# Eight single orders in a hand-scheduled transformer block: query copies, first scores, last probabilities, first casts of up and down, sums near the end

## The chip, the cores and the metric

The kernel is one program on one core of a Trainium2 chip. The time is that of a whole execution on the device, in microseconds (us); of several executions the median is taken. The engines are TensorE (PE, matrix products into PSUM banks), VectorE (DVE), ScalarE (ACT), GpSimd (POOL) and SyncE (SP, which issues most of the DMA transfers). Each runs its own list of instructions in order and waits on semaphores for the others.

## The reference

One layer of a diffusion backbone over 512 latent tokens of width 2048, with 256 context tokens, all in float32:

```python
h = modulate(rms_norm(x), sh_a, sc_a)                    # the context likewise
q_a, kv_a, k_rope, gate_b, gate_c, hc = split(h @ w_in)
q = rope(rms_norm(q_a) @ w_q_b)                          # 8 heads of 128 + 64
k, v = rms_norm(kv_a) @ w_kv_b                           # latent and context tokens
att = softmax(q @ k.T * scale) @ v                       # 512 rows against 512 + 256 keys
conv = gate_b * dwconv3(gate_c * hc)
x = x + gt_a * (group_rms_norm(concat(att, conv)) @ w_out)
h = modulate(rms_norm(x), sh_f, sc_f)
a, g = split(dwconv3(h @ w_up))                          # 2 x 5504 columns
x = x + gt_f * ((a * silu(g)) @ w_down)
return rms_norm(x, g_final)
```

## The kernel before

**Numbers.** PE takes float32 in a rounded form (fp32r). So each factor is split into a high and a low part, and a product is three matmuls: high by high, high by low, low by high (`mm3`, L202 to L204; `mm2`, L210 to L212, takes two factors that lie side by side). Such a split (`split`, `split4`, `hilo`) is a cast of ACT, named with an h at its end (`wk0h`, `dw00h`), and a subtraction of DVE, named with an l (`wk0l`, `dw00l`), which needs the cast. A matmul of L202 waits for the cast, that of L204 (low weights) or L203 (low data) for the subtraction. The casts' buffers rotate: a new one waits until PE has read an old one.

**Stages**, one after the other: the input projection (0 to 384 us of the trace), the attention (384 to 612), the output projection (612 to 790), the first product of the MLP, "up" (790 to 1647), and the second, "down" (1647 to the end). Up and down are done with seven products of blocks instead of eight, so sums of weight blocks are made first (DVE, and DMAs of POOL that add to what lies there).

**Order.** Each engine's order is set when the program is built: a scheduler places the instructions by its own costs, in the order in which the code was written where nothing else speaks. `tc.issue_after(i)` asks, without a wait at run time, that what is written under it comes later than `i` on the engine of `i`. `keep` holds written order, and the list `behind` puts the first matmul of the next `mm3` after a given one. `bg`, `drain` and `pump` run side work piece by piece.

**PSUM in the attention.** `sml` gives one of four single banks, `big` one of two pairs of banks. Scores of one step (one head, 128 rows) fill a pair (`scores`, L1012 to L1025: five matmuls of 512 columns over the latent keys and five of 256 over the context keys). `softmax` takes the minimum on DVE (`mn`, L1035) and the exponential on ACT (`p`, L1038), which frees the pair. `transposes` (L1043) turns the probabilities with PE in two halves (`t`, L1053; three 128-column matmuls each), and splits them into `pth` (ACT, L1056) and `ptl` (DVE, L1057). `attend` multiplies these by the values (`po`). `s02` is the score tile of head 0, step 2; `pth` and `ptl` carry no step in the profile. `rms` (L359) normalizes the context's keys: sums of squares over partitions by two one-column matmuls from `kct` (L343), a square root, a reciprocal, a spread by transposes (L324) and a copy `kcr` (L356), in one pair of banks from `big`.

**Side work there.** `q_nope`, `q_rope`, `k_nope`, `values` prepare the next pair of heads; `xq` (L934) is the copy of the queries that are rotated (`qr`, L409), `wk` and `wv` the split weights of keys and values. `late_both` (L1127) does dot products of the modulation on DVE (L281). `gb` are spreads of the convolution's norms, merged by DVE (`acc`, L404). After the loop, `out_row` (L1202) splits the first mixed rows (`mx`) and starts the output projection (`of`).

**First rows of up.** `first_weights` (`ufw0` to `ufw5`) and `hf_tile` (L1257 on) make the factors of the first products `uf`. `hf_early` (L1278) makes those of the first half of the tokens for the rows 0 to 2 as side work of the last output column `ol`. A second norm (`rms_steps` over `fq`) runs beside them.

**First weights of down.** `finish` (L1543) does the last two products `q4` and `q3` of a column group of up. After the last group (42) down begins: it splits `dw00` and multiplies it with `yl0`, read back by SP (`y_load`) in a high and a low part, into the banks `d00` to `d07`.

**Last groups of down.** `weights_of` (L1646) loads four blocks of a group and adds them (`v23s`, L1660; a POOL DMA, L1661, adds a fourth block). `d_p2` (L1718) ends with two sums, `a11` and `a12` (L1722, L1723), from which the weights of the product `p6` are cast; `d_q4` and `d_q3` are the last products of the group before, `ended` its end. Groups are numbered 0 to 23: `v21q4` are weights of group 21, `v23s` a sum of group 23.

## Time and profile before

| what | value |
|---|---|
| time, median of 3 runs | 2112.55 us (2111.74 to 2114.03) |
| the profiled execution's own time | 2109.51 us |
| its span, first to last instruction | 2107.7 us |
| granted TensorE clock, mean | 0.998 |
| PE busy | 2080.4 us (99%) |
| DVE busy | 1792.8 us (85%) |
| ACT busy | 1100.6 us (52%) |
| POOL busy | 126.8 us (6%) |
| DVE busy from 384 to 612 us | 178.21 of 228 us |

A row of the timeline gives the start, the duration, the engine, the line, the operation, what it writes and reads and, in brackets, how long the engine was idle before it and who ended that. Names stand without buffer numbers there: `s` is any score tile, `hf` any split row. Rows merged into one say how many (x2). A matmul's duration holds a pipeline of which the next one overlaps a part, so the spacing of two starts tells more than the duration: 512 columns start 0.23 us apart, 256 columns 0.12 us. The list of waits sums idle time by the pair of instructions, that which waited and that which ended it.

### The profile page before, as it was taken

The numbers are of one execution on the slowest core, as the hardware profiler recorded it, in microseconds if no ns is written. First come the engines' busy times: TensorE is split into PE (matmuls) and PEld (weight loads), VectorE is DVE, ScalarE is ACT, GpSimd is POOL, SyncE is SP. The second block draws the span as 40 slices with busy tenths as digits, with TensorE's granted clock in tenths as the row PEclk, the third lists the DMA queues.
The fourth block names the chain that finished last, engine by engine and source line by source line (L and its number), as shares of the span: only waits on it lengthen the run. The fifth ranks groups of instructions, "written<-read, shape, count | busy, mean of one in ns | idle before, by whom it ended". The sixth has DMA issues, their size and how long they took to land.

```text
span 2107.7 us, 35339 instructions
## 1 busy us (share of the span) xinstructions
PE 2080.4 (99%) x13304; PEld 1875.2 (89%) x13304; DVE 1792.8 (85%) x2911; ACT 1100.6 (52%) x1815; POOL 126.8 (6%) x161
## 2 busy tenths in 40 slices
PE   8999999999999999999999999999999999999997
PEld 6787888888888889999999999999999889999997
DVE  7888987788777879898999899999999659888887
ACT  6675454655552237555555555555555333333445
POOL 0000000000000000110000000000000000000000
PEclk9999999999999999999999999999999999999999
DMA  9899997445538966677888878888888989878684
GB/s 336 295 342 323 326 331 256 138 144 194 195 140 326 346 222 181 168 217 207 243 227 229 243 221 236 244 226 229 241 227 232 362 302 315 251 231 240 202 247 135
DMA packets 166606, 514.78 MB, mean 244 GB/s; under 512 B 18722, under 2 KB 23074, under 8 KB 157346
## 3 DMA queue, kind: packets, MB, share of 16 engines
q1 hardware_dynamic: 127744, 407.90, 56.4%
q0 software_dynamic: 19312, 70.40, 15.7%
q10 hardware_dynamic: 19378, 34.23, 4.3%
q8 instruction: 104, 1.70, 0.3%
q14 instruction: 68, 0.55, 0.1%
HBM read 465.26 MB, written 46.14 MB: 243 GB/s over the span
## 4 chain that ended last, share of the span: by engine, by line
PE 87%; DVE 5%; DMA 4%; issue 2%; ACT 2%; POOL 0%; DVEq 0%; POOLq 0%; ACTq 0%; SPq 0%
PE pp L202 3%; PE pp L204 3%; PE pp L203 3%; DMA rw<-in_w_in 2%; PE o L202 1%; PE o L204 1%; PE o L203 1%; PE d L202 1%; PE d L203 1%; PE d L204 1%; PE uf L202 1%; PE uf L203 1%; PE uf L204 1%; PE of L202 1%; PE of L204 1%
## 5 line engine op out<-in xcount | busy, mean ns | idle before, releaser
L1460 POOL DMA_DIRECT2D u_s<-in_w_up x80 | 68.4, 855 | 680.5 <-DMA u_s<-in_w_up 405.2
L285 DVE SCALAR_TENSOR_TENSOR ada<-ada,sv 128x2048 f32<-128x2048 f32 x33 | 75.4, 2285 | 7.0 <-DMA ada<-in_w_ada 6.7
L671 DVE SCALAR_TENSOR_TENSOR ada<-ada,svc 128x1024 f32<-128x1024 f32 x64 | 77.1, 1217 | 2.8 <-DMA ada<-in_w_ada 2.8
L181 ACT CAST w_0h<-rw 128x512 fp32r<-128x512 f32 x50 | 30.7, 620 | 69.5 <-PE pp L203 33.5
L1581 DVE TENSOR_TENSOR u<-u,u_s 128x1024 f32<-128x1024 f32 x40 | 48.7, 1218 | 3.5 <-DMA u_s<-in_w_up 3.4
L256 DVE SCALAR_TENSOR_TENSOR ada<-ada,sv 128x1024 f32<-128x1024 f32 x40 | 48.3, 1217 | 3.2 <-DMA ada<-in_w_ada 3.2
L1582 DVE TENSOR_TENSOR u<-u,u 128x1024 f32<-128x1024 f32 x40 | 48.6, 1215 | 0.0
L182 DVE TENSOR_TENSOR w_0l<-rw,w_0h 128x512 fp32r<-128x512 f32 x50 | 34.0, 685 | 8.5 <-ACT w_0h L181 7.7
L1380 DVE TENSOR_TENSOR tp<-a,tp 128x256 fp32r<-128x256 f32 x90 | 37.4, 416 | 2.8 <-ACT tp L1379 2.8
L1035 DVE TENSOR_REDUCE mn<-s 128x1 f32<-128x768 f32 x32 | 30.5, 952 | 10.9 <-PE s L1024 10.9
L1379 ACT CAST tp<-a 128x256 fp32r<-128x256 f32 x90 | 35.7, 403 | 6.3 <-DMA yl6h<-y_d 3.7
L1085 POOL TENSOR_TENSOR gr<-gr,half 128x8 f32<-128x8 f32 x4 | 10.3, 2580 | 474.9 <-DVE gr L1084 427.8
L281 DVE SCALAR_TENSOR_TENSOR ra<-ra,sv 128x1024 f32<-128x1024 f32 x32 | 38.0, 1216 | 0.0
L1056 ACT CAST pth<-t 128x384 fp32r<-128x384 f32 x64 | 28.6, 485 | 16.8 <-PE t L1053 16.6
L1343 ACT ACTIVATE g<-g 128x512 f32<-128x512 f32 x43 | 27.3, 634 | 17.8 <-DVE g L1337 17.5
L1057 DVE TENSOR_TENSOR ptl<-t,pth 128x384 fp32r<-128x384 f32 x64 | 33.1, 547 | 3.3 <-ACT pth L1056 3.3
L1335 ACT ACTIVATE g<-cg,sm 128x512 f32<-128x512 f32 x40 | 32.6, 815 | 0.0
L1335 ACT ACTIVATE a<-ca,sm 128x512 f32<-128x512 f32 x40 | 32.1, 802 | 0.0
L683 ACT COPY acc<-pp 128x512 f32<-128x512 f32 x49 | 28.3, 580 | 5.3 <-PE pp L204 5.3
L1038 ACT ACTIVATE p<-s,mn 128x768 f32<-128x768 f32 x32 | 29.3, 915 | 3.2 <-DVE mn L1035 3.2
L1336 DVE SCALAR_TENSOR_TENSOR g<-cg,sm,g 128x511 f32<-128x511 f32 x40 | 29.8, 745 | 0.0
L1336 DVE SCALAR_TENSOR_TENSOR a<-ca,sm,a 128x511 f32<-128x511 f32 x40 | 29.8, 744 | 0.0
(10502 smaller groups left out, 8997.6 us busy)
## 6 DMA issues: line engine op xcount, KB each, us to landing
ada<-in_w_ada SPq DMA_DIRECT2D x128, 512.0 KB, 6.1
u<-in_w_up SPq DMA_DIRECT2D x120, 512.0 KB, 9.1
w<-t_d SPq DMA_DIRECT2D x161, 256.0 KB, 5.4
u_s<-in_w_up SPq DMA_DIRECT2D x80, 512.0 KB, 3.9
u_s<-in_w_up POOLq DMA_DIRECT2D x80, 512.0 KB, 9.8
ada<-in_w_ada SPq DMA_DIRECT2D x33, 1024.0 KB, 6.3
t_d<-tp ACTq DMA_DIRECT2D x126, 256.0 KB, 6.0
v<-in_w_dnw SPq DMA_DIRECT2D x72, 384.0 KB, 5.6
```

The lines of the kernel that those rows point to most:

```text
L202: PE.matmul(ps, w[0], x[0], start=first, stop=False, skip_group_check=on_top)
L203: PE.matmul(ps, w[0], x[1], start=False, stop=False, skip_group_check=on_top)
L204: PE.matmul(ps, w[1], x[0], start=False, stop=last, skip_group_check=on_top)
L256: ins = V.scalar_tensor_tensor(out=r, in0=r, scalar=1.0, in1=vec[:, i * 1024:(i + 1) * 1024], op0=ALU.mult, op1=ALU.mult, accum_out=col[:, ...
L281: keep(V.scalar_tensor_tensor(out=halves[i], in0=halves[i], scalar=1.0, in1=svs[i], op0=ALU.mult, op1=ALU.mult, accum_out=lc[:, t % 4:t % ...
L285: keep(V.scalar_tensor_tensor(out=r, in0=r, scalar=1.0, in1=sv, op0=ALU.mult, op1=ALU.mult, accum_out=mod[:, t:t + 1]))
L671: keep(V.scalar_tensor_tensor(out=raw[q], in0=raw[q], scalar=1.0, in1=svc[:, q * 1024:(q + 1) * 1024], op0=ALU.mult, op1=ALU.mult, accum_o ...
L1335: A.activation(u, src, AF.Identity, bias=s("fb", m), scale=s("fw", 86 + m))
L1336: V.scalar_tensor_tensor(out=u[:, 1:], in0=src[:, :T - 1], scalar=s("fw", m), in1=u[:, 1:], op0=ALU.mult, op1=ALU.add)
L1460: G_.dma_start(r[-1], src[more], accum_op=ALU.add)
L1581: V.tensor_tensor(out=a11, in0=a11, in1=s1, op=ALU.add)
L1582: V.tensor_tensor(out=a12, in0=a12, in1=a11, op=ALU.add)
```

## The change

No arithmetic is changed. Eight places get another order:

1. First scores, (a): the context keys' norm takes a single bank (`one=width < T`) instead of a pair. (b): `late_both` is written after the first softmax. (c): the next head pair's first product `q_nope(1, 0)` is put behind the last matmul of the second score tile.
2. Copies of rotated queries: `drain()` is put behind the first copy `xq0`, and in later pairs the splits of `wk` and `wv` behind the copy before them.
3. A side piece of the step n = 31 is put behind the last `ptl`.
4. Last probabilities: the first four `out_row` are put behind the last `pth` and `ptl`.
5. First casts of up: row 2 (`hf_tile(2, H0)`) leaves the side work and goes behind the first two splits of weights.
6. First cast of down: the split `dw00` is made inside the last `finish`, between its product `q4` and the activation that follows.
7. Sums near the end: for group 23, the sum `v23s` and its DMAs are written after `d_q4` of group 21,
8. and the two sums of group 22 as well as the end of a group before (`ended`) after that.

```diff
@@ -357,7 +357,7 @@
         yield pb[:, :width]
 
     def rms(sqs, n, width, dst):
-        for _ in rms_steps(sqs, n, 0, width, dst):
+        for _ in rms_steps(sqs, n, 0, width, dst, one=width < T):
             pass
 
     def hilo(src, n, nm, width=512):
@@ -931,13 +931,13 @@
                 Q[2 * pr + i] = hilo(ps, T, f"q{pr}{i}")
                 return
             xq = t2([P, T], F32, f"xq{pr}")
-            A.copy(out=xq, in_=ps)
+            xq_copied[:] = [A.copy(out=xq, in_=ps).ins]
             if pr:
                 q_rope(pr, xq)
             else:
                 q_rope_0.append(xq)
 
-        q_rope_0 = []
+        q_rope_0, xq_copied = [], []
 
         def q_rope(pr, xq):
             rope(xq, sml(f"qr{pr}"), f"qr{pr}")
@@ -952,8 +952,9 @@
         def k_nope(pr, i):
             if i == 0:
                 raw = wkv["kv"]
-                wkv["k"] = split(raw, 0, 512, f"wk{pr}")
-                wkv["v"] = split(raw, 512, 512, f"wv{pr}")
+                with tc.issue_after(xq_copied[0]) if pr else ExitStack():
+                    wkv["k"] = split(raw, 0, 512, f"wk{pr}")
+                    wkv["v"] = split(raw, 512, 512, f"wv{pr}")
             w = wkv["k"]
             psl = sml(f"pkl{pr}{i}")
             for k in range(2):
@@ -1009,6 +1010,8 @@
             return [(q_nope, pr, 0), (q_nope, pr, 2), (k_nope, pr, 0), (q_nope, pr, 1), (k_nope, pr, 1),
                     (values, pr, 0), (values, pr, 1), (values, pr, 2)]
 
+        scored = []
+
         def scores(st):
             hd, tt = st
             kl, kcx = K[hd]
@@ -1021,7 +1024,7 @@
                 PE.matmul(d, qh[:, tsl], klo, start=False, stop=False)
                 PE.matmul(d, ql[:, tsl], kh, start=False, stop=False)
                 PE.matmul(d, QR[hd][:, tsl], rh_, start=False, stop=False)
-                PE.matmul(d, QR[hd][:, tsl], rl_, start=False, stop=True)
+                scored[:] = [PE.matmul(d, QR[hd][:, tsl], rl_, start=False, stop=True).ins]
             return ss
 
         den, oo, PT = {}, {}, {}
@@ -1038,7 +1041,7 @@
             A.activation(pt, ss[:, :768], AF.Exp, bias=mn, scale=-1.0, accum_out=den[hd // 2][:, i:i + 1])
             return pt
 
-        ptl_last = []
+        pth_last, ptl_last = [], []
 
         def transposes(st, pt):
             hd, tt = st
@@ -1053,7 +1056,7 @@
                     PE.transpose(tr[:, kb * P:(kb + 1) * P], pt[:, (3 * u + kb) * P:(3 * u + kb + 1) * P], ident)
                 trv = tr[:, :384].rearrange("p (k t) -> p k t", k=3)
                 hi = pth[:, 3 * u:3 * u + 3, bs]
-                A.copy(out=hi, in_=trv)
+                pth_last[:] = [A.copy(out=hi, in_=trv).ins]
                 ptl_last[:] = [V.tensor_tensor(out=ptl[:, 3 * u:3 * u + 3, bs], in0=trv, in1=hi.bitcast(F32), op=ALU.subtract).ins]
 
         def attend(hd, half):
@@ -1107,7 +1110,8 @@
             q_nope(0, i)
         q_rope(0, q_rope_0[0])
         bg.extend(ctx_prep(g) for g in range(CTX_EARLY, 8))
-        drain()
+        with tc.issue_after(xq_copied[0]):
+            drain()
         bg.extend(post)
         for i in range(3):
             ctx_tile(i)
@@ -1124,11 +1128,12 @@
         late_load(ada_raw)
         for f, i in ((k_ctx, 0), (k_ctx, 1), (values, 2)):
             f(0, i)
-        late_both(ada_raw)
         out_raw = {}
         steps = [(hd, tt) for hd in range(NH) for tt in range(4)]
         ss = [scores(steps[0]), scores(steps[1])]
         pt = softmax(steps[0], ss[0])
+        late_both(ada_raw)
+        behind.append(scored[0])
         q_nope(1, 0)
         fetch(1, 1)
         for g in late_bg[:4]:
@@ -1150,7 +1155,8 @@
                 merge(n // 8 - 1)
             late_dot(1)
             if n > 24 and n % 2:
-                deque(late_bg[4 + (n - 25) // 2], 0)
+                with tc.issue_after(ptl_last[0]) if n == 31 else ExitStack():
+                    deque(late_bg[4 + (n - 25) // 2], 0)
 
             at = n % 8
             if at == 0 and n and n < 24:
@@ -1206,7 +1212,8 @@
         for k in range(OUT_EARLY):
             if k % 2 == 0:
                 w = row_weights(w_out_first, k, "of", raw=out_raw[k])
-            out_row(k, w)
+            with tc.issue_after(pth_last[0]), tc.issue_after(ptl_last[0]):
+                out_row(k, w)
         merge(3)
         drain()
 
@@ -1276,7 +1283,7 @@
         hf_last[:] = hf_last[1], ins.ins
 
     def hf_early():
-        for j in range(3):
+        for j in range(2):
             hf_tile(j, HS[0])
             yield
 
@@ -1475,6 +1482,8 @@
         residual(NK - 1, ps, HS[1])
     one_bank[0] = in_turn([6])
     bg.append(rms_steps(fsq, D, T // 2, T // 2, rl, wait=(1, 1), one=True, pin=True))
+    with tc.issue_after(first_two[0]), tc.issue_after(first_two[1]):
+        hf_tile(2, H0)
     held += [first_weights(k, k > 2) for k in range(2, EARLY)]
     with tc.issue_after(first_two[0]), tc.issue_after(first_two[1]):
         for k in range(3, EARLY):
@@ -1540,9 +1549,10 @@
         A.copy(out=r, in_=ps[:, :256])
         return r
 
-    def finish(st):
+    def finish(st, between=lambda: None):
         f, a22, s4, u2, u3, pa, pc, cg, ca = st
         product(pa, a22, "4", f"u{f}q4", False)
+        between()
         A.activation(ca[:, H0], pa[:, :256], AF.Identity, scale=-1.0)
         beside(ca[:, H0], pa, True)
         product(pc, s4, "22", f"u{f}q3", False)
@@ -1595,7 +1605,12 @@
         if first_acts:
             acts(*first_acts.pop(0))
         pend = f, a22, a12, u2, u3, pa, pc, cg, ca
-    finish(pend)
+    dw = {}
+
+    def down_first():
+        dw[0, 0] = split4(fetched.popleft(), 1024, "dw00")
+
+    finish(pend, down_first)
 
 
     phc.close()
@@ -1643,7 +1658,7 @@
     class Step:
         pass
 
-    def weights_of(st):
+    def weights_of(st, whole=True):
 
         z = Step()
         z.st, z.win, z.m = st, window(st), 2 * (st % 8)
@@ -1657,9 +1672,15 @@
         SP.dma_start(z.a11, src[0])
         SP.dma_start(z.s1, src[2])
         SP.dma_start(z.a12, src[1])
-        V.tensor_tensor(out=z.s3, in0=z.a11, in1=z.s1, op=ALU.add)
-        G_.dma_start(z.s1, src[3], accum_op=ALU.add)
-        SP.dma_start(z.a22, src[3])
+
+        def rest():
+            V.tensor_tensor(out=z.s3, in0=z.a11, in1=z.s1, op=ALU.add)
+            G_.dma_start(z.s1, src[3], accum_op=ALU.add)
+            SP.dma_start(z.a22, src[3])
+
+        z.rest = rest
+        if whole:
+            rest()
         return z
 
     y_load(0)
@@ -1671,7 +1692,7 @@
             plain_fetch()
             if h == 0 and k + 2 < STD:
                 y_load(k + 2)
-            w = split4(fetched.popleft(), 1024, f"dw{h}{k}")
+            w = dw.pop((h, k), None) or split4(fetched.popleft(), 1024, f"dw{h}{k}")
             for i in range(8):
                 mm3(ps[i], part(w, i), y[k], k == 0, k == STD - 1)
             pump(1)
@@ -1715,9 +1736,13 @@
         seven(z, z.pa, z.a11, "11", "p1", True)
         into(z, 0, H0, z.pa)
 
-    def d_p2(z):
+    def d_p2(z, sums=True):
         seven(z, z.pb, z.a12, "21", "p2", True)
         into(z, 0, H0, z.pb)
+        if sums:
+            d_sums(z)
+
+    def d_sums(z):
         with tc.issue_after(last_lo[0]):
             V.tensor_tensor(out=z.a11, in0=z.a11, in1=z.s1, op=ALU.add)
         V.tensor_tensor(out=z.a12, in0=z.a12, in1=z.a11, op=ALU.add)
@@ -1819,18 +1844,23 @@
                 win_load(*first.pop(0)) if first else None
         if prev is not None:
             d_q3(prev)
-            ended(prev)
+            if st < STEPS - 3:
+                ended(prev)
             if prev.st in (STEPS - 6, STEPS - 5):
                 j = 2 * (prev.st - STEPS + 6)
                 with tc.issue_after(last_hi[0]):
                     scaled[0][j] = scale_out(j, 0, True)
         d_p7(z)
-        prev = z
-
-    za, zb = nxt, weights_of(STEPS - 1)
+        before, prev = prev, z
+
+    za, zb = nxt, weights_of(STEPS - 1, False)
     d_p1(za)
-    d_p2(za)
+    d_p2(za, False)
     d_q4(prev)
+    with tc.issue_after(last_lo[0]):
+        zb.rest()
+        ended(before)
+    d_sums(za)
     d_p1(zb)
     d_p2(zb)
     d_p6(za)
```

What the scheduler makes of it is read from the lists of instructions. First PE, where the first scores are prepared: `pkl` are keys of a head, `pv` values, `rs<-io,kct` the sums of squares of the context's norm, `s` score tiles. Before:

```order
L995 MATMUL pv_3991<-wv0h,kl0h 128x256
L996 MATMUL pv_3991<-wv0l,kl0h 128x256
L343 MATMUL rs<-io,kct 128x1 x2
L997 MATMUL pv_3991<-wv0h,kl0l 128x256
L995 MATMUL pv_3991<-wv0h,kl1h 128x256
L996 MATMUL pv_3991<-wv0l,kl1h 128x256
L997 MATMUL pv_3991<-wv0h,kl1l 128x256
L1020 MATMUL s_4059<-kl00h,q00h 128x512
```

And now, at the place of the same two matmuls:

```order
L203 MATMUL pkl_3934<-kl1l,wk0h 128x512
L204 MATMUL pkl_3934<-kl1h,wk0l 128x512
L343 MATMUL rs<-io,kct 128x1 x2
L202 MATMUL pkl_3955<-kl0h,wk0h 128x512
L203 MATMUL pkl_3955<-kl0l,wk0h 128x512
L204 MATMUL pkl_3955<-kl0h,wk0l 128x512
L202 MATMUL pkl_3955<-kl1h,wk0h 128x512
```

The two matmuls stood shortly before the first scores; now they stand 26 rows further up, behind the six matmuls of the first key tile.

Then PE a little later, at the end of the fourth score tile: `s_4182` is `s03`, `t_4170` and `t_4176` are the transposed probabilities of step 1 (those of step 0, `t_4139` and `t_4145`, stood ahead of `s03` before), `pq` is a product of side work, `s_4246` is `s10`. Before:

```order
L1022 MATMUL s_4182<-kcx_4023,q00l 128x256
L1023 MATMUL s_4182<-krc,qro0h 128x256
L1024 MATMUL s_4182<-krc,qro0h 128x256
L1053 MATMUL t_4170<-io,p_4135 128x128 x3
L1053 MATMUL t_4176<-io,p_4135 128x128 x3
L202 MATMUL pq_4197<-qa0h,wq12h 128x512
L203 MATMUL pq_4197<-qa0l,wq12h 128x512
```

And now:

```order
L1026 MATMUL s_4182<-krc,qro0h 128x256
L1027 MATMUL s_4182<-krc,qro0h 128x256
L1056 MATMUL t_4139<-io,p_4078 128x128 x3
L1056 MATMUL t_4145<-io,p_4078 128x128 x3
L1056 MATMUL t_4170<-io,p_4135 128x128 x3
L1056 MATMUL t_4176<-io,p_4135 128x128 x3
L1023 MATMUL s_4246<-kl01h,q01h 128x512
```

Both steps' transposes now follow `s03` directly, and `s10` follows them without the 12 matmuls of `pq` between. On ACT the exponential `p02`, which frees the pair of banks for `s10`, stands behind the two casts `pth` of step 0 in both lists.

Last DVE, near the end: `c11` is a running sum of the result, `v2211` and `v2212` the sums `a11` and `a12` of group 22, `ssq` sums of squares for the last norm. Before:

```order
L1722 TENSOR_TENSOR v2211_22124<-v2211_22124,v22s1_22125 128x768
L384 TENSOR_TENSOR ssq_17429<-ssq_17429,eq80_22290 128x512
L1660 TENSOR_TENSOR v23s3_22324<-v2311_22321,v23s1_22322 128x768
L1708 SCALAR_TENSOR_TENSOR c11_18119<-v21a_22135,gn_95,c11_18119 128x256
L1723 TENSOR_TENSOR v2212_22126<-v2212_22126,v2211_22124 128x768
L1329 TENSOR_TENSOR v21q4l_22384<-v2122_21928,v21q4h_22383 128x768
```

And now:

```order
L1729 SCALAR_TENSOR_TENSOR c11_18119<-v21a_22135,gn_95,c11_18119 128x256
L1336 TENSOR_TENSOR v21q4l_22373<-v2122_21928,v21q4h_22372 128x768
L1677 TENSOR_TENSOR v23s3_22318<-v2311_22315,v23s1_22316 128x768
L384 TENSOR_TENSOR ssq_17433<-ssq_17433,eq80_22400 128x512
L1747 TENSOR_TENSOR v2211_22124<-v2211_22124,v22s1_22125 128x768
```

The subtraction `v21q4l` moved ahead of `v23s3` and of both sums of group 22. `v23p1l`, `v23p2l`, `v2311` and `v22p6l`, which come later, keep their order among themselves, but two of the moved operations (a `ssq` and `v2212`) now stand between `v23p1l` and `v23p2l`.

## Prediction

> **What bounds the kernel now.** I read the page's head first, then the clock, then the list of waits of PE, and then the timeline at each place where the change touches a wait.
>
> ```profile
> PE 2080.4 (99%) x13304; PEld 1875.2 (89%) x13304; DVE 1792.8 (85%) x2911; ACT 1100.6 (52%) x1815; POOL 126.8 (6%) x161
> core 0: 2107.7 us, clock 0.998
> ```
>
> PE is busy for all but 27.3 us of the span, and the clock is whole. The change removes no matmul, so it can only win where PE stands still, and it loses where it makes PE stand still. Only the waits that PE itself shows count; an order that is better for DVE or ACT and ends no wait of PE is worth nothing. Four of those that the eight edits may touch are these (us in total, times, longest):
>
> ```profile
> PE qr L409 <- ACT xq L934: 1.7, 2, 1.0
> PE v21a L204 <- DVE v21q4l L1329: 0.9, 1, 0.9
> PE s L1020 <- ACT p L1038: 0.7, 2, 0.5
> PE uf L202 <- ACT ufw0h L1328: 0.7, 1, 0.7
> ```
>
> Three more, of 0.46, 1.09 and 1.02 us, stand in rows below. Together that is 6.6 us, 0.31% of the time. A measurement of this kernel can tell about 0.2% (4.2 us) from no change. So even a full success is only just visible, and each place must be asked what is late next.
>
> A wait also costs a restart: below, the first matmul after one starts 0.34 us before its follower, where two such matmuls without a wait are 0.23 apart. I add 0.11 us to each wait that goes or comes. [...]
>
> **First scores.**
>
> ```profile
> 416.83 0.39 PE L202 MATMUL pkl<-kl0h,wk0h 128*128 128x512 f32 x1
> 417.06 0.40 PE L203 MATMUL pkl<-kl0l,wk0h 128*128 128x512 f32 x1
> 419.05 0.43 DVE L384 TENSOR_TENSOR kct<-kct,kc 128x256 f32<-128x256 f32 x1 [0.47 <-ACT kc L383]
> 424.90 0.50 PE L1020 MATMUL s<-kl00h,q00h 128*128 128x512 f32 x1 [0.46 <-ACT kcr L356]
> 425.24 0.40 PE L1021 MATMUL s<-kl00l,q00h 128*128 128x512 f32 x1
> ```
>
> Two waits go: the pair of banks no longer waits for the norm's copy `kcr` (0.46), and `s02` now follows `pq10` and three spreads, so that `p00` is done in time (0.5, the longer of the two waits for `p` in the list). With two restarts that is -1.2 us.
>
> Two come. The norm's two matmuls now follow the six of the first key tile: PE is there at 416.83 + 6 x 0.233 = 418.23, but `kct` ends at 419.05 + 0.43 = 419.48, on lists of ACT and DVE that are the same up to there. That is 1.25 + 0.11 = +1.36 us.
>
> The second is `s10`. Its pair of banks is freed by `p02`, which stands on ACT behind both casts `pth` of step 0:
>
> ```profile
> 437.83 0.86 ACT L1056 CAST pth<-t 128x384 fp32r<-128x384 f32 x2 [0.66 <-PE t L1053]
> 439.55 0.90 ACT L1038 ACTIVATE p<-s,mn 128x768 f32<-128x768 f32 x1 [0.86 <-DVE mn L1035]
> 440.35 0.19 ACT L1038 ACTIVATION_READ_ACCUMULATOR p<-s,mn 128x1 f32 x1
> 439.72 0.82 PE L1053 MATMUL t<-io,p 128*128 128x128 f32 x6
> ```
>
> From the start of the transposes, the first of them needs about 0.35 us, the casts 0.86, `p` and its reading 0.99: 2.2 us. PE has 12 transposes until `s10`, at 0.109 each (my spacing from the row of six: 0.82 less the last one's own 0.27, by 5) 1.3 us. The wait is 0.9 + 0.11 = +1.0 us. Before, `pq12` (12 matmuls of 512 columns, 2.8 us) covered it. The place as a whole: +1.36 + 1.0 - 1.2 = +1.2 us; from -1.2 (neither wait comes) to +1.6.
>
> **Copies of rotated queries.** There are two waits, of 1.0 and 0.7 us. The first, `xq0`, is to be met by putting `drain()` behind the copy; but the lists of ACT and of PE around it are the same row by row, so I give it nothing. For the second:
>
> ```profile
> 493.42 0.62 ACT L181 CAST wk2h<-rk 128x512 fp32r<-128x512 f32 x1 [1.93 <-DMA rk<-in_w_kv]
> 494.47 0.58 ACT L934 COPY xq<-pq 128x512 f32<-128x512 f32 x1
> 495.10 0.70 PE L409 MATMUL qr<-xq,kc 128*128 128x512 f32 x1 [0.70 <-ACT xq L934]
> ```
>
> ACT idled 1.93 us for the DMA with the copy queued behind. Now the copy comes first, in that idle time, and `wk2h` still starts when its data is there. -0.8 us, from -0.8 to -0.6.
>
> **Last probabilities.**
>
> ```profile
> 604.17 0.62 ACT L366 CAST mx0h<-acc 128x512 fp32r<-128x512 f32 x1
> 604.68 0.86 ACT L1056 CAST pth<-t 128x384 fp32r<-128x384 f32 x2
> 606.09 1.02 DVE L1057 TENSOR_TENSOR ptl<-t,pth 128x384 fp32r<-128x384 f32 x2
> 606.69 0.39 PE L203 MATMUL po<-ptl,v30h 128*128 128x256 f32 x1 [1.09 <-DVE ptl L1057]
> ```
>
> On ACT the casts `pth` now stand ahead of `mx0h`, on DVE `ptl` ahead of `acc` and `mx0l`. The first cast ends at 604.17 + 0.48 = 604.65 and the first `ptl`, 0.55 long with its handover, at 605.2: L203 starts at 605.25 instead of 606.69, -1.44 us. What is pushed back, `mx0h` to 605.6 and `mx0l` to 606.9, is needed by `of` at about 608.2. -1.45 us, from -1.6 to -0.9. The order given to the piece at n = 31 hides in DVE's idle time: 0.
>
> **First casts of up.**
>
> ```profile
> 791.21 0.83 ACT L1328 CAST ufw0h<-ufr 128x768 fp32r<-128x768 f32 x1
> 791.46 0.48 DVE L1287 SCALAR_TENSOR_TENSOR x<-ol,mod,x 128x256 f32<-128x256 f32 x1 [0.89 <-PE ol L204]
> 798.79 0.40 ACT L1248 CAST hf<-x 128x256 fp32r<-128x256 f32 x1
> 799.25 0.74 PE L202 MATMUL uf<-hf,ufw_0h 128*128 128x256 f32 x4
> ```
>
> With row 2 gone from ahead of it, `ufw0h` is done 1.4 us earlier and the wait of 0.7 goes. But in the rows before, PE reaches row 3 (`hf`, L1248) at 799.25, just after its cast ends at 799.19: the next limit is already there. Row 2's work now stands on ACT and DVE between 793.6 and 796.8. ACT's chain starts, as before, from the last column of `ol` at 791.46, and adding up its casts in the new order puts the end of row 3's cast at 799.2 again. DVE, which had made row 2's parts in idle time, is 0.3 us later there, while the two transposes of the second norm now fall into PE's wait (0.2 us). So what PE wins at 791 it waits for in front of row 3: 0 us, from -0.8 to +0.4.
>
> **First cast of down.**
>
> ```profile
> 1643.91 1.05 ACT L1328 CAST u42q3h<-u 128x1024 fp32r<-128x1024 f32 x1 [0.38 <-PE u42c L211]
> 1646.76 1.05 ACT L1328 CAST dw00h<-d 128x1024 fp32r<-128x1024 f32 x1 [1.79 <-PE u42a L203]
> 1647.86 0.50 PE L202 MATMUL d<-yl0h,dw00h 128*128 128x512 f32 x1 [1.02 <-ACT dw00h L1328]
> 1641.26 0.38 SPq L1641 DMA_DIRECT2D yl0h<-y_d  x1
> yl0l<-y_d SPq DMA_DIRECT2D x1, 256.0 KB, 5.7
> ```
>
> The two casts change places, and so buffers: `dw00h` comes at 1643.91, `u42q3h` at 1646.76, still 6 us ahead of its product. PE could go on 1.02 + 0.11 earlier, at 1646.73; `yl0h`, if it takes as long as `yl0l`, the load behind it, lands at 1641.26 + 5.7 = 1646.96. So -0.9 us. On SP, a load for group 0 now stands ahead of the loads of `yl5` and waits for the subtraction `dw05l`:
>
> ```profile
> 1671.40 1.22 DVE L1329 TENSOR_TENSOR dw05l<-d,dw05h 128x1024 fp32r<-128x1024 f32 x1 [1.16 <-ACT dw05h L1328]
> yl5h<-y_d SPq DMA_DIRECT2D x1, 256.0 KB, 6.4
> 1681.55 0.63 PE L202 MATMUL d<-yl5h,dw05h 128*128 128x512 f32 x2
> ```
>
> That ends 0.9 us earlier, at 1671.7; three loads later, at an estimated 0.5 us each, `yl5h` is issued at 1673.2 and lands at 1679.6, 1.0 us before its use, which is also 0.9 earlier. It holds, with little to spare: from -1.2 to -0.4.
>
> **Sums near the end.**
>
> ```profile
> 2062.12 0.95 DVE L1329 TENSOR_TENSOR v21q4l<-v,v21q4h 128x768 fp32r<-128x768 f32 x1
> 2066.65 0.96 DVE L1722 TENSOR_TENSOR v<-v,v23s 128x768 f32<-128x768 f32 x1 [0.45 <-DMA v23s<-in_w_dnw]
> 2067.92 0.95 DVE L1329 TENSOR_TENSOR v22p6l<-v,v22p6h 128x768 fp32r<-128x768 f32 x1
> 2069.63 0.28 PE L204 MATMUL v22a<-w,v22p6l 128*128 128x256 f32 x1
> ```
>
> `v21q4l` now runs ahead of the sums, and PE wins the 0.9 + 0.1. SP's and POOL's lists are the same there, so no transfer moves. It then meets `v22p6l`: that follows, now as before, a sum that waits for a DMA until 2066.65, and ends at 2068.87. Before, PE came there at 2069.63; now it would be there at 2068.6 and starts at 2068.92. -0.7 us, from -1.0 to -0.3.
>
> **The sum.** +1.2 - 0.8 - 1.45 + 0 - 0.9 - 0.7 = -2.65 us. The profiled execution took 2109.51 us, 1.8 more than its span, so it would come to 2106.9; it was 3.04 us below the median of 2112.55, and against the median I predict 2109.9, which is -0.13%.
>
> **The rivals.**
>
> *The new waits do not come* (0.27). The two new waits are worked out from the lists, not seen. If PE arrives later at both, because other small things hold it, they vanish: -2.65 - 2.36 = -5.0, 2107.5 us; with the 0.8 of the first casts of up as well, 2106.7. For it speaks that DVE and ACT have room in the attention (178.21 and 127.81 us busy of 228, the third and fourth engine of the row below), so that a chain may be quicker than mine; against it that both waits end with rows whose place in the lists is fixed.
>
> ```profile
> 384.00:612.00 228.00, 223.08 (x1496) 201.17 (x1495) 178.21 (x325) 127.81 (x275) 6.70 (x3) 1.00 0.45 153
> u<-in_w_up SPq DMA_DIRECT2D x120, 512.0 KB, 9.1
> ```
>
> *Late rows in down* (0.13). If `yl5h` takes 9.1 us, as the loads of `u` do in the last row above, it lands at 1682.3, 1.7 us after its use, and `yl5l` and the rows behind it half a microsecond later still: 2109.9 + 2.2 = 2112.1, no change. That it took 6.4 before, and `yl0l` 5.7, speaks against it.
>
> *The wait for `p` repeats* (0.08). The wait of `s10` behind the casts is a pattern: scores that follow transposes directly wait 1.0 us for `p`. If the seven steps after it, up to 485 us, each show it, +7 us: 2116.9, slower. From three repeats on the gain is gone. For it speaks that ACT has the casts ahead of `p` at each step; against it that `pq12`, `po` and `pq11`, of 2 to 3 us each, stand between in the next steps.
>
> [...]
>
> **The numbers.** The forecast has 0.52, the three rivals 0.27, 0.13 and 0.08. Over 0.2% faster means below 2108.3: the first rival, 0.27. Over 0.2% slower, above 2116.8: the third, 0.08. The rest, 0.65, is within 0.2%. The range goes from 2106.5, the first rival with the gain in up, to 2112.8, the second with half a microsecond more; only the third and what is beyond these ends is left out.
>
> **What would show it.** Right: in the profile after, PE waits about 1.3 us for `kct` at `rs` (L343 before) near 418 us and about 0.9 us at `s10` near 440; `qr` keeps one wait of 1.0; `po` L203 waits 0.4; `uf` waits near 799 instead of 792; `d` waits for `yl0h` or not at all; `v22a` waits 0.3 for `v22p6l`. The forecast is wrong if PE shows neither of the two first waits, if `uf` L202 shows no wait in row 3, or if `s` waits for `p` more than twice after 440 us.

## The result, and the profile after

| what | before | after |
|---|---|---|
| time, median | 2111.06 us | 2107.62 us |
| ratio to before, 95% interval | | 0.9985 [0.9979, 0.9991] |
| span of the profiled execution | 2107.7 us | 2105.3 us |
| DVE busy | 1792.8 us | 1792.3 us |

Both medians are of 21 executions taken side by side. One execution of the kernel before took 11654 us; the ratio and its interval go by the others. The change makes the kernel 0.15% faster, by the interval between 0.09% and 0.21%; the forecast was 0.13%. The head of the page and the clock of the changed kernel:

```profile
PE 2080.1 (99%) x13304; PEld 1874.9 (89%) x13304; DVE 1792.3 (85%) x2911; ACT 1101.3 (52%) x1815; POOL 125.2 (6%) x161
core 0: 2105.3 us, clock 0.998
```

PE's busy time is the same as before to 0.3 us, and the clock is as whole as before. So nearly the whole difference is in PE's waits. Its list of waits after the change (us in total, times, longest):

```profile
PE rs L343 <- DVE kct L384: 1.2, 1, 1.2
PE s L1023 <- ACT p L1041: 1.1, 2, 0.9
PE qr L409 <- ACT xq L934: 1.0, 1, 1.0
PE rs L324 <- DVE rr L316: 1.0, 2, 0.6
PE t L1056 <- DVE o L1098: 0.5, 2, 0.2
PE v22a L204 <- DVE v22p6l L1336: 0.3, 1, 0.3
PE v23b L204 <- DVE v23p2l L1336: 0.3, 1, 0.3
PE v1a L204 <- DVE v1q4l L1336: 0.3, 1, 0.3
PE po L203 <- DVE ptl L1060: 0.2, 1, 0.2
```

These of the old waits are gone or much shorter: the second of `qr` for `xq` (of the 1.7 us one wait of 1.0 is left), `po` for `ptl` (1.1 to 0.2), `d` for `dw00h`, `v21a` for `v21q4l`, `uf` for `ufw0h`, `s` for `kcr` and, not named by the prediction, `pq` for `kl30l` near 553 us (0.4). In their place stand shorter ones and two long ones, the two that the prediction had worked out from the lists. The timeline of the changed kernel shows both, and behind them the last probabilities, row 3 of up and the first product of down:

```profile
417.64 0.40 PE L204 MATMUL pkl<-kl1h,wk0l 128*128 128x512 f32 x1
418.69 0.43 DVE L384 TENSOR_TENSOR kct<-kct,kc 128x256 f32<-128x256 f32 x1 [0.48 <-ACT kc L383]
419.26 0.58 PE L343 MATMUL rs<-io,kct 128*128 128x1 f32 x4 [1.23 <-DVE kct L384]
...
437.51 0.95 DVE L1038 TENSOR_REDUCE mn<-s 128x1 f32<-128x768 f32 x1
439.18 0.86 ACT L1059 CAST pth<-t 128x384 fp32r<-128x384 f32 x2 [1.85 <-PE t L1056]
439.93 0.92 ACT L1041 ACTIVATE p<-s,mn 128x768 f32<-128x768 f32 x1
440.99 0.50 PE L1023 MATMUL s<-kl01h,q01h 128*128 128x512 f32 x1 [0.86 <-ACT p L1041]
...
604.46 0.86 ACT L1059 CAST pth<-t 128x384 fp32r<-128x384 f32 x2
605.21 0.63 ACT L366 CAST mx0h<-acc 128x512 fp32r<-128x512 f32 x1
605.59 0.38 PE L203 MATMUL po<-ptl,v30h 128*128 128x256 f32 x1 [0.21 <-DVE ptl L1060]
...
797.48 0.40 ACT L1255 CAST hf<-x 128x256 fp32r<-128x256 f32 x1
797.74 0.43 PE L324 MATMUL rs<-io,rr 128*128 128x128 f32 x2 [0.41 <-DVE rr L316]
797.93 0.74 PE L202 MATMUL uf<-hf,ufw_0h 128*128 128x256 f32 x4
...
1640.08 0.38 SPq L1656 DMA_DIRECT2D yl0h<-y_d  x1
1642.73 1.05 ACT L1335 CAST dw00h<-d 128x1024 fp32r<-128x1024 f32 x1 [0.38 <-PE u42c L211]
1645.50 1.56 PE L202 MATMUL d<-yl0h,dw00h 128*128 128x512 f32 x6
```

At 419 us PE waits 1.23 us for `kct` (worked out: 1.25), at 441 us `s10` waits 0.86 us for `p02`, which runs on ACT behind the two casts `pth` (worked out: 0.9). ACT took its rows in the order of its list here: the minimum of `p02` (`mn`) was there at 438.46 us, yet ACT stood idle until 439.18 (1.85 us in all), when the transposes let the casts ahead of it start, and `p02` came behind them at 439.93. At 605 us `pth` stands ahead of `mx0h`, and L203 waits 0.21 us instead of 1.09. At 798 us PE waits 0.41 us for the spread of the norm (`rr`), just ahead of row 3, whose cast is done 0.05 us before the row starts. At 1645 us `d` starts without a wait.

Where PE stands at the same matmul in both profiled executions says what each stretch won. The start times of those matmuls, and what the prediction gave to the stretch that ends there:

| PE arrives at | before | after | won so far | in this stretch | forecast |
|---|---|---|---|---|---|
| `qr` of `xq0` (nothing changed up to here) | 396.99 | 396.62 | 0.37 | 0.37 | 0 |
| last side product of the attention (`pq31`): first scores and query copies | 553.36 | 553.59 | -0.23 | -0.60 | -0.4 |
| first `of`: last probabilities | 609.62 | 608.51 | 1.11 | 1.34 | 1.45 |
| `hf4h` of up: first casts of up | 801.70 | 800.52 | 1.18 | 0.07 | 0 |
| first `d`: first cast of down | 1647.86 | 1645.50 | 2.36 | 1.18 | 0.9 |
| first `v21a`: the inside of down | 2042.16 | 2039.61 | 2.55 | 0.19 | 0 |
| first `v23c`: sums near the end | 2085.98 | 2083.50 | 2.48 | -0.07 | 0.7 |

The sum, 2.48 us, is close to the forecast 2.65. But 0.37 us of it lies in a part that nothing touches, the end gave nothing, and the first row hides two errors that cancel, as the experiments show.

### The profile page after: what moved, and what is told of

The parts are those of the page before. It is cut to its first block, busy times and chain, and to the rows that moved or that the text cites. A ratio compares the mean times of both kernels' runs of the same rounds, so it can differ in the third digit from the quotient of the medians.

```text
span 2105.3 us, 35333 instructions
## 1 busy us (share of the span) xinstructions
PE 2080.1 (99%) x13304; PEld 1874.9 (89%) x13304; DVE 1792.3 (85%) x2911; ACT 1101.3 (52%) x1815; POOL 125.2 (6%) x161
## 4 chain that ended last, share of the span: by engine, by line
PE 89%; DVE 4%; DMA 3%; issue 2%; ACT 2%; POOL 0%; DVEq 0%; SPq 0%; POOLq 0%; ACTq 0%
PE pp L202 4%; PE pp L204 4%; PE pp L203 4%; PE o L203 1%; PE o L202 1%; PE o L204 1%; PE d L203 1%; PE d L202 1%; PE d L204 1%; PE of L203 1%; PE of L202 1%; PE of L204 1%; PE uf L203 1%; PE uf L204 1%; PE uf L202 1%
```

## The experiments

Theory: each place is worth the waits it takes from PE less those it brings, and the places add. Rival: a lead of PE is given back at the next limit, so that the places do not add. Where a time rests on one execution, only the trace is used, since single executions of this kernel differ by several us for reasons elsewhere, as shown below.

**First scores alone.** Of the change, only the three edits of place 1 on the kernel before:

```diff
-        for _ in rms_steps(sqs, n, 0, width, dst):
+        for _ in rms_steps(sqs, n, 0, width, dst, one=width < T):
...
-        late_both(ada_raw)
         out_raw = {}
...
         pt = softmax(steps[0], ss[0])
+        late_both(ada_raw)
+        behind.append(scored[0])
         q_nope(1, 0)
```

> Only the three orders of the first scores are applied to the kernel before. Theory (a wait removed is worth its length less that of what is late next): PE waits about 1.2 us for kct near 418 us and 0.9 us for p at s10 near 441 us, the waits for kcr (0.46) and for p00 (0.47) are gone; from the first key tile to the second pair's rotated query PE takes 1.1 us longer than in the kernel before, and the span is about 1 us longer. Rival (each removed wait is worth its length, and the two new waits come from the other orders): no wait for kct, span 1.2 us shorter.

Measured: 2111.42 us against 2110.27, ratio 1.0005 [0.9996, 1.0014]. The two new waits are there with 1.23 and 0.86 us, and the two old ones are gone. Counted from `xq0`, PE is 1.0 us later than before at 453 us. Then comes a wait that was not expected:

```profile
456.29 0.50 PE L202 MATMUL pq<-qa0h,wq11h 128*128 128x512 f32 x1 [0.41 <-DVE kl10l L367]
```

With it PE is 1.5 us later at 478 us. At `pq31` it is only 0.47 us later (553.68 - 553.36, and 0.16 that it was earlier at `xq0`). The reason is `qr` at 495 us: as PE comes later, it no longer finds `xq` late, and that wait of 0.70 us is gone without any edit there. So the edits cost PE 1.5 us up to that point, and 0.5 us after the next wait has taken its share. (In the whole change the wait for `kl10l` is not there, and PE is 1.16 us later at 478 us.)

**Query copies alone.** Only place 2:

```diff
+                with tc.issue_after(xq_copied[0]) if pr else ExitStack():
...
-        drain()
+        with tc.issue_after(xq_copied[0]):
+            drain()
```

> Of the changed kernel only the copies of rotated queries: drain() and the splits of wk and wv behind the copy before them. If a place is worth the waits it removes: the wait of qr for xq near 495 us (0.70 and the restart) goes, that near 396 (1.0) stays, PE is 0.8 us earlier behind 495 us, and no other wait between 384 and 612 us moves by more than 0.2 us. If the scheduler's other orders follow the lead of PE, a wait of 0.2 to 0.4 us at t for o (L1095 before) or for the splits wk and wv takes a part of it, and 0.4 to 0.6 us are left at 552 us.

Measured: the wait of `qr` near 495 us goes, as expected, and PE is 1.0 us earlier there (492.36, against 495.10 before and a lead of 1.75 us that this execution had from the start). Five microseconds later 0.3 us of it is left, and by 514 us nothing. The timeline of this kernel:

```profile
494.83 0.62 ACT L181 CAST wq21h<-rq 128x512 fp32r<-128x512 f32 x1 [1.91 <-DMA rq<-in_w_q]
495.35 0.85 ACT L1057 CAST pth<-t 128x384 fp32r<-128x384 f32 x2
496.09 0.92 ACT L1039 ACTIVATE p<-s,mn 128x768 f32<-128x768 f32 x1
497.15 0.50 PE L1021 MATMUL s<-kl11h,q11h 128*128 128x512 f32 x1 [0.55 <-ACT p L1039]
```

ACT stands 1.91 us for the DMA of the next weights (`wq21h`) with `pth` and `p` queued behind that cast, and the score tile waits 0.55 us for `p`. It is the same pattern as the one removed 2 us earlier, a cast that waits for a load ahead of what PE needs. A small wait of `t` for `o` (0.23 us at 551) comes, and the old one of `pq31` for `kl30l` (0.41) goes. The lead at `pq31` is 1.77 us, against 1.75 at `xq0`: the edit is worth nothing by itself. (In this execution loads came late in the output projection: PE waited 1.36 and 1.80 us there, the clock was half for 3.41 us behind the second wait, as told at the end, and PE lost 5.6 us between 767 and 792 us in all. The edit touches nothing there, so the time of 2115.84 us says nothing of it.)

**All without the first scores.** The changed kernel with the three edits of place 1 undone.

> The changed kernel without its three orders of the first scores (the other five places as changed). Theory: the waits for kct and at s10 go, those for kcr and p00 (0.46 and 0.47) come back; the span is 1.1 us shorter than that of the changed kernel (about 2104.2), the ratio to the kernel before about 0.998. Rival (the place gains, and the two waits would have come anyway): span 1.2 us longer than the changed kernel's.

Measured: 2108.15 us against 2110.27, ratio 0.9986 [0.9977, 0.9994], about the ratio of the whole change. In the trace `kcr` (0.46 us) and `p00` (0.47 us) are waited for again, `kct` and `s10` are not, and a new wait stands at 499 us:

```profile
499.15 0.50 PE L1021 MATMUL s<-kl11h,q11h 128*128 128x512 f32 x1 [0.76 <-ACT p L1039]
```

That is the give-back of the query copies again. At `pq31` this kernel is 0.21 us behind the one before, the changed kernel 0.60: undoing a place that shows +1.2 us of waits is worth 0.4 us. The span of the profiled execution is 2104.2 us, as the theory had it, but not for its reason: when the last groups of down begin, this kernel is 2.60 us ahead of the one before, the changed kernel 2.55. The rest is won in the sums near the end, which are ordered as in the changed kernel and here show no wait (below).

**Last probabilities alone.** Places 3 and 4:

```diff
-            out_row(k, w)
+            with tc.issue_after(pth_last[0]), tc.issue_after(ptl_last[0]):
+                out_row(k, w)
```

> Of the changed kernel only the last probabilities: the first four out_row behind the last pth and ptl, and the piece of n = 31 behind ptl. If a place is worth the waits it removes: the wait of po (L203) for ptl near 606 us falls from 1.09 us to 0.2, PE is 1.3 us earlier from there on, and the span is 1.3 us below that of before. If instead the gain is given back at the next limit, the first matmul of of or of the later rows waits for mx0h or mx0l by about 1 us, and PE's lead at the start of up (790 us) is under 0.4 us. The wait of d for dw00h (1.02) and that of v21a for v21q4l (0.9) stay.

Measured: PE's place against the kernel before moves from 5.31 us behind at `pq31` to 3.97 at `of`, a gain of 1.34, and at the first `ol` products it is still 3.97. Nothing is given back. In all eight kernels that have this edit the same stretch wins 1.30 to 1.36 us. Of the lag of 5 us, 1.9 us were there at 340 us; most of the rest came from a late load, for which the first `qr` waited 2.52 us, and from the clock behind that wait (told at the end), so the time of this one execution, 2115.49 us, says nothing.

**First cast of down alone.** Place 6:

```diff
+    def down_first():
+        dw[0, 0] = split4(fetched.popleft(), 1024, "dw00")
+
+    finish(pend, down_first)
```

> Of the changed kernel only the first cast of down: dw00 is split inside the last finish. If a place is worth the waits it removes: d (L202) near 1646.7 us shows no wait for dw00h, PE is 1.2 us earlier from there on (1.0 of wait and 0.16 of restart), and yl5h is not waited for. If yl0h sets the next limit, d waits for that DMA until about 1646.9 and the gain is 0.9. If the load for group 0 delays the rows of y (a rival of the prediction), yl5 waits 1 to 2 us near 1680.

Measured: `d` starts at 1647.10 without a wait. Against the kernel before, PE goes from 0.42 us behind to 0.76 ahead, 1.18 us, and at `v23c` it is 0.82 ahead. `yl0h` is no limit, `yl5h` is not waited for. The place keeps what it wins. In none of the eight kernels that have this edit does `d` wait.

**First casts of up alone.** Place 5:

```diff
-        for j in range(3):
+        for j in range(2):
             hf_tile(j, HS[0])
...
+    with tc.issue_after(first_two[0]), tc.issue_after(first_two[1]):
+        hf_tile(2, H0)
```

> Only the order of the first casts of up is applied. Theory: the wait of 0.67 us at the first uf goes, and PE waits instead in front of the norm's spread and of row 3 (about 0.4 and 0.1 us); row 4 (hf4h) starts within 0.2 us of the kernel before, counted from the last column's first matmuls. Rival (the removed wait is worth its length): row 4 starts 0.8 us earlier and no wait stands in front of row 3.

Measured: the wait for `ufw0h` is gone, and row 3 now waits 1.07 us for its own cast. The timeline of this kernel:

```profile
798.71 0.74 PE L202 MATMUL uf<-hf,ufw_0h 128*128 128x256 f32 x4 [1.07 <-ACT hf L1248]
```

So not 0.4 and 0.1 us as expected, but one wait, and a longer one. From `of` to `hf4h` PE loses 0.4 us (ahead by 1.16, then by 0.74). What is won at 791 us is lost again 7 us later. This execution also ran slower through down, which is told at the end.

**Sums near the end alone.** Places 7 and 8, the diff as in the change.

> Only the orders of the sums near the end are applied. The prediction's step (the sum that waits for the DMA of group 23 stays at its time): v22p6l ends at its old time, PE gains 0.7 us there. Rival (the sum of group 23 itself comes later because it stands behind v21q4l and the DMA behind it too, and two more operations ahead of v23p2l cost PE 0.5): PE gains 0.1 us at most, and waits about 0.34 us for v23p2l and 0.35 for v22p6l. A third way (the DMA was late in the changed kernel only because PE arrived 2.5 us earlier): as the prediction's step, with no wait over 0.35 and a gain of 0.7.

Measured: the wait for `v21q4l` is gone, and two come: `v23b` for `v23p2l` (0.27) and `v22a` for `v22p6l` (0.61). PE is 0.70 us behind before the place and 1.11 behind after it. The edit wins nothing here. In the changed kernel the same is seen; DVE and PE there:

```profile
2057.84 0.96 DVE L1677 TENSOR_TENSOR v23s<-v,v23s 128x768 f32<-128x768 f32 x1 [1.24 <-DMA v23s<-in_w_dnw]
...
2061.45 0.69 DVE L384 TENSOR_TENSOR ssq<-ssq,eq 128x512 f32<-128x512 f32 x1
2062.05 0.96 DVE L1748 TENSOR_TENSOR v<-v,v 128x768 f32<-128x768 f32 x1
2063.31 0.95 DVE L1336 TENSOR_TENSOR v23p2l<-v,v23p2h 128x768 fp32r<-128x768 f32 x1
2064.79 0.96 DVE L1747 TENSOR_TENSOR v<-v,v23s 128x768 f32<-128x768 f32 x1 [0.52 <-DMA v23s<-in_w_dnw]
2066.06 0.95 DVE L1336 TENSOR_TENSOR v22p6l<-v,v22p6h 128x768 fp32r<-128x768 f32 x1
...
2064.32 0.38 PE L204 MATMUL v23b<-w,v23p2l 128*128 128x256 f32 x1 [0.34 <-DVE v23p2l L1336]
2067.06 0.39 PE L204 MATMUL v22a<-w,v22p6l 128*128 128x256 f32 x1 [0.35 <-DVE v22p6l L1336]
```

`v23p2l` stands behind a sum of squares (`ssq`) and the sum `a12` of group 22 (L1748) that the change put ahead of it, and `v22p6l` behind the sum of group 23 (L1747) that waits for a DMA. Before, that sum started at 2066.65, now at 2064.79, 1.86 us earlier; PE is 2.5 us earlier.

**The end with one more step.** The changed kernel, with the second sum of group 22 and both sums of group 23 written behind `p6` of group 22:

```diff
-    d_sums(za)
+    d_sums(za, 1)
     d_p1(zb)
-    d_p2(zb)
+    d_p2(zb, False)
     d_p6(za)
+    d_sums(za, 2)
+    d_sums(zb)
```

> The changed kernel with one more step at the end: of group 22 the second sum, and of group 23 both sums, are written behind the product p6 of group 22, so that on DVE v23p2l and v22p6l stand ahead of them. Theory: these subtractions were late because each was queued behind a sum, the second one behind a sum that waits for a DMA; then the waits of v23b for v23p2l (0.34) and of v22a for v22p6l (0.35) go, nothing waits more than 0.3 us between 2055 and 2085 us, and PE is 1.0 us earlier at the end than in the changed kernel. Rival: the DMA is late for everything in that stretch; then v21q3l, v23p6l or v22p7l, which stand behind the moved sums, are waited for by 0.5 us or more, and under 0.4 us is won.

Measured: DVE in this kernel:

```profile
2061.39 0.95 DVE L1336 TENSOR_TENSOR v23p2l<-v,v23p2h 128x768 fp32r<-128x768 f32 x1
2062.65 0.95 DVE L1336 TENSOR_TENSOR v22p6l<-v,v22p6h 128x768 fp32r<-128x768 f32 x1
2064.39 0.95 DVE L1748 TENSOR_TENSOR v<-v,v23s 128x768 f32<-128x768 f32 x1
```

Both subtractions run ahead of the sum, which now comes when its data is there. PE shows no wait between 2055 and 2078 us, and from `v21a` to `v23c` it wins 0.99 us on the kernel before (3.55 to 4.54 us ahead), where the changed kernel lost 0.07. In both kernels the transfer of POOL for which the sum of group 23 waits landed equally late, 25.04 us after the first `v21a` here and 25.08 in the changed kernel. So, with the transfer late, the queue position decides whether `v22a` waits.

But the position alone does not make PE wait. *All without the first scores* has the same orders near the end as the changed kernel; there the transfer landed 24.00 us after `v21a`, neither of the two waits came, and from `v21a` to `v23c` PE took 42.82 us, as here. The kernel before took 43.81. Over all kernels this stretch took 43.11 to 44.41 us with the old order (six executions), 43.74 to 44.23 with that of the change in five executions and 42.82 in the sixth, 42.82 and 43.23 with that of this section. Single executions thus differ by as much as the edit wins; the waits that go or stay are the better sign. The time is 2106.08 us against 2109.89, ratio 0.9983 [0.9974, 0.9992], which cannot be told from the 0.9985 of the change.

**Up with another order of casts.** The changed kernel, with the casts of row 3 ahead of the weights of row 4, and so on:

```diff
-    held += [first_weights(k, k > 2) for k in range(2, EARLY)]
-    with tc.issue_after(first_two[0]), tc.issue_after(first_two[1]):
-        for k in range(3, EARLY):
-            hf_tile(k, H0)
+    for k in range(2, EARLY):
+        held.append(first_weights(k, k > 2))
+        if k > 2:
+            with tc.issue_after(first_two[0]), tc.issue_after(first_two[1]):
+                hf_tile(k, H0)
```

> The changed kernel with the casts of row 3 of up (hf30) put ahead of the split weights of row 4, and those of row 4 ahead of row 5. Theory: what the change wins at the first uf it loses again because row 3's cast stands behind the weights of rows 4 and 5; then the two small waits near 798 and 799 us (0.41 for rr, 0.1 in row 3) shrink together to under 0.2 us and the rows behind are 0.3 to 0.8 us earlier. Rival: the weights of rows 4 and 5 are the limit themselves; then uf waits for ufw_0h or ufw_512h of row 4 or 5 by 0.3 us or more, and nothing is won, or up to 0.5 us lost.

Measured: row 3's cast and its first product in this kernel:

```profile
795.24 0.41 ACT L1255 CAST hf<-x 128x256 fp32r<-128x256 f32 x1
...
797.43 0.64 PE L202 MATMUL uf<-hf,ufw_0h 128*128 128x256 f32 x4
```

The cast stands at 795.24 instead of 797.48, and both waits are gone. (The spread of the norm, which waited for `rr`, now also stands behind row 3.) PE keeps the whole gain of the first `uf`: ahead of the kernel before by 1.83 us at `uf` and 1.89 at `hf4h`, where the changed kernel goes from 2.10 to 1.18. That is 1.0 us, more than expected. At the end little is left of it: waits of `v1a` for a running sum (0.24) and for `v1q4l` (0.30), of `v18a` for `v18q4l` (0.40) and of `v22a` for `v22p6l` (0.83) take it back, and PE is 2.30 us ahead at `v23c`, the changed kernel 2.48. The time is 2107.10 us, ratio 0.9989 [0.9979, 0.9998], no better than the change itself.

**First scores without the two new waits, in two steps.** First, `rs` behind the second key tile and `s10` behind `pq12`, by order alone:

```diff
-            f(0, i)
-            pump(1)
+            with tc.issue_after(spread_last[0]) if f is values and i else ExitStack():
+                f(0, i)
+            pump(f is values or i)
...
-                ss[n % 2] = scores(steps[n + 2])
+                with tc.issue_after(turned[0]) if n == 2 else ExitStack():
+                    ss[n % 2] = scores(steps[n + 2])
```

> The changed kernel with its two new waits at the first scores taken away by order alone: the norm's two matmuls rs stand behind the second key tile, as no side work is run behind the first, the values behind the norm's spread, and the scores s10 behind the last matmul of pq12. If these two waits are what the change loses (the theory): PE shows no wait of more than 0.3 us for kct near 419 us and for p near 441 us, is 2.2 to 2.5 us ahead of the changed kernel from 450 us on, the span is about 2103.0 us and the median 2105.2 (0.9989 of the changed kernel, 0.9974 of the one before). If the wait only moves (the rival): kcr or a later p is waited for by 0.5 us or more, and the lead behind 450 us is under 1.2 us. If a lead in the attention is given back at later limits that a DMA sets, the lead at 450 us is over 2 us and the span is still above 2104 us.

Measured: `rs` waits no more. At 442 us the wait has only moved:

```profile
441.48 1.01 DVE L1063 TENSOR_TENSOR ptl<-t,pth 128x384 fp32r<-128x384 f32 x2
...
442.08 0.50 PE L202 MATMUL pq<-qa0h,wq12h 128*128 128x512 f32 x1 [1.05 <-DVE ptl L1063]
```

The four halves of the transposes of steps 0 and 1 fill all four single banks, and `pq12` needs the first of them, which `ptl` frees. Then the second step: the score tile `s03` also goes behind the transposes of step 0, where it stood in the kernel before.

```diff
+                after = turned[0] if n == 2 else t_first[0] if n == 1 else None
+                with tc.issue_after(after) if after else ExitStack():
+                    ss[n % 2] = scores(steps[n + 2])
```

> As scores_fixed, but with the transposes of step 0 put back ahead of the score tile s03, where they stood in the kernel before. Theory: pq12 waited 1.05 us in scores_fixed because the transposes of both steps together take all four single banks, and its bank is freed only by ptl; with the first two made 1 us earlier no bank is late. Then neither rs, pq12 nor s10 waits more than 0.3 us, PE is 2.3 us ahead of the changed kernel behind 500 us (scores_fixed: 1.1), and the median is about 2105.3. Rival: the transposes of step 0 now wait for p00 by 0.5 us or more, as in the kernel before, and the lead stays under 1.8 us.

Measured: `pq12` waits 0.21 us, `s10` not at all. But at 499 us the give-back is there again:

```profile
440.15 0.50 PE L202 MATMUL pq<-qa0h,wq12h 128*128 128x512 f32 x1 [0.21 <-DVE ptl L1063]
...
499.00 0.50 PE L1026 MATMUL s<-kl11h,q11h 128*128 128x512 f32 x1 [0.76 <-ACT p L1044]
```

At `qr` near 494 us this kernel is 1.9 us ahead of the changed one (each against its own `xq0`), at `pq31` 1.1 us, as much as the first step. The expected 2.3 is nearly reached (2.2 at 467 us) and then half lost. The times are 2105.12 us (ratio 0.9980 [0.9971, 0.9989]) and 2105.45 us (0.9983 [0.9975, 0.9992]). That they come out at the expected 2105.2 and 2105.3 does not bear out the theory, as only half of the lead arrived.

**The three mended places together.**

> scores_fixed2, end2 and up2 together. If each place is worth the waits it removes, they add: 2.3 + 1.0 + 0.5 = 3.8 us against the changed kernel, 2103.8 us, 0.9966 of the kernel before. If a lead is given back at limits that DMAs set, the sum is under 2.5 us, 2105 us or more.

Measured: 2104.23 us against 2109.89, ratio 0.9977 [0.9968, 0.9985]. In the trace, each against its own `xq0`, PE is 0.9 us ahead of the changed kernel at `pq31`, 2.0 at `hf4h`, 1.9 when the loop of down starts, 0.3 at `v22a` and 1.6 at `v23c`. So the rival holds: 1.6 us of the 3.8 arrive, and down takes 1.6 of the lead before the mended end gives 1.3 back. The ledger is from one execution, the slowest of the eleven (2108.44 us); the ratios, 0.9977 against 0.9985, say 1.7 us. By the point estimates this is the fastest kernel made here, though its interval still overlaps that of the change.

What takes leads in down is best seen in the changed kernel, where `v1a` waits for the first time:

```profile
1756.97 0.96 DVE L1747 TENSOR_TENSOR v<-v,v2s 128x768 f32<-128x768 f32 x1 [2.24 <-DMA v2s<-in_w_dnw]
1758.92 0.96 DVE L1336 TENSOR_TENSOR v1q4l<-v,v1q4h 128x768 fp32r<-128x768 f32 x1
1759.93 0.39 PE L204 MATMUL v1a<-w,v1q4l 128*128 128x256 f32 x1 [0.30 <-DVE v1q4l L1336]
```

The sum of group 2 waits 2.24 us for a DMA. In the kernel before it starts at 1757.54 without a wait, so it moved by 0.57 us where PE moved by 2.73. The subtraction `v1q4l` is queued behind it.

## Why the prediction was right, and where it was not

The time came out as forecast (2107.62 against 2111.06, a ratio of 0.9985; forecast 0.9987), in part by luck, since several of its terms were off and their errors cancelled. Of the rivals none took place: both new waits came (the first rival said they would not), `yl5` did not wait, and `s` waits for `p` twice, 1.1 us in all, not after every step; the second of these, 0.25 us at 595 us, was there before too. The absolute 2107.62 lies 2.3 us below the forecast 2109.9 and beside the first rival's 2107.5, but that does not speak for the rival: the trace shows both waits, and the kernel before, too, measured 1.5 us less than the 2112.55 that the forecast was taken from.

- *First scores, +1.2.* The two new waits had the predicted size (1.23 and 0.86 for 1.25 and 0.9), and the local sum is +1.16 (PE's delay at 478 us, counted from `xq0`). The step that failed is that this sum goes through to the end: `qr` at 495 us waits for a copy whose time a DMA sets (in the kernel before, ACT stood 1.93 us for it with the copy queued behind), and in *First scores alone* that wait went without an edit and took 1.0 us of the delay (from 1.44 to 0.47). Alone, the place costs 0.47 us.
- *Query copies, -0.8.* The wait went as said, but "what is late next" was not asked. It is `p`, behind the cast of `wq21h` that waits 1.91 us for a DMA: alone, the place is worth 0.0 us. The two errors are the same one seen from both sides, and that they cancelled is luck: +0.4 was forecast for both, +0.60 measured.
- *Last probabilities, -1.45.* Right, in mechanism and size: -1.34, in the change and alone.
- *First casts of up, 0.* Right in size (0.07), and row 3's cast is the next limit as said. But the sign that was given for it, a wait of `uf` L202 in row 3, did not come: of what PE won, 0.41 us of wait fell one instruction earlier, to the norm's spread, and row 3 then starts 0.05 us behind its cast. Alone the place costs 0.4 us, with the wait in row 3; with the casts in another order the same place wins 1.0.
- *First cast of down, -0.9.* The mechanism was right, the size too small: 0.23 us was taken off the term because `yl0h` was taken to land 5.7 us after its issue. It was issued at 1640.08 and was there at 1645.50, so 1.18 us were won. The late rows did not come.
- *Sums near the end, -0.7.* Wrong for the changed kernel: no gain. The failed step is "so no transfer moves", on which the time of the sum ahead of `v22p6l` rests. The sum waits for a transfer of POOL that starts behind the first sum of group 23; it came 1.86 us earlier than before while PE came 2.5 earlier, so that it was 0.7 us later against PE and took the gain. From issue to landing this transfer took 5.36 us instead of 5.08 (5.05 to 5.91 in the eight kernels with an order of the sums other than before, 4.82 to 5.10 in the six others); why is open. Of the two operations that the lists showed to be put ahead of `v23p2l`, the rows of 0.69 and 0.96, none was priced either; they make `v23b` wait, but not the total: in *Up with another order of casts* `v23b` does not wait, `v22a` waits 0.83 us instead, and the stretch is as long to 0.15 us. Where the transfer landed early (*All without the first scores*), the place won 1.0 us.
- *Not foreseen:* small waits in the loops (`t` for `o`, `v1a` for `v1q4l`), 0.2 to 0.3 us each. `v1q4l` stands behind the sum that waits 2.24 us for a DMA. Ahead of `o` DVE stands for no DMA: in the changed kernel it idled 0.48 and 0.50 us for the scores of PE a few rows before, at 500.55 and 549.48 us. What made `o` late was not shown.

What stays open: how much of the 0.37 us won before 397 us, where nothing is changed, is due to the change at all. Other kernels with the same beginning arrive there between 395.24 and 400.47 us, so it is most likely chance, and the ratio of the medians is the better measure. Nor can differences of 0.2 us in the attention be read from single executions: in *First cast of down alone* and *First casts of up alone*, where nothing there is changed, `qr` waits 0.94 and 0.92 us near 495 us instead of 0.70, and PE loses 0.22 us between `xq0` and `pq31`.

## What to carry to other kernels

Price a removed wait by what is late next on the engines that feed PE, not by its length: where a cast or a sum that waited for a DMA stood in the same list, a lead of PE was lost there (0.7 of 1.0 us in *Query copies alone*, with a cast that waited 1.91 us), and a delay of PE was absorbed there (1.44 us fell to 0.47 in *First scores alone*), so such terms did not add: in *The three mended places together* 1.6 of 3.8 us arrived. A gain held where the next operands depend on PE's own progress (last probabilities, 1.34 us; first cast of down, 1.18 us), or, as far as two executions show it, where what waits for a DMA is moved behind what PE needs (the end with one more step, 0.99 and 0.58 us). After mending an order, look again at what now stands in front of the next two operands, and read single executions by PE's place at named matmuls, since their total times (2106.04 to 2111.95 us for the changed kernel) differ by more than such edits are worth.
